# Three first products in quarters, and two more pairs of kept T blocks, in a Strassen-like matmul with leaky ReLU

## The chip, the cores and the metric

One core of one Trainium2 chip runs the whole kernel. The time is device time in microseconds (us) from start to end of one execution; a kernel's time is the median of several executions. One execution is also recorded by the hardware profiler; its span runs from the first to the last instruction.

## The reference

```python
a = randn(4096, 4096) float32;  b = randn(4096, 4096) float32;  alpha = 0.01
x = np.matmul(a, b)
return np.where(x > 0, x, alpha * x)
```

## The kernel before

**Tiling.** Both matrices are cast to 16 bits. `out` is cut into 4 groups of 1024 rows (g) and 4 pairs of 1024 columns (j). A region (g, j) is one 1024x1024 block of `out`, with the inner dimension of 4096 cut in two halves of 2048, each again in two units k = 0, 1 of 1024 (8 chunks of 128 rows). Region (0, 0) is done by plain products. The other 15 run in the order of `regions`: (0, 1), (0, 2), (0, 3), then in each of groups 1 and 2 the pairs 2, 0, 3, 1, and in group 3 the pairs 2, 0, 1, 3. A *turning* region is the last of its group: it also brings in the A blocks of the next one.

**A region** is one step of the Winograd form of Strassen's scheme. A group has the blocks A11, A12, A21, A22 and sums S1 to S4 of them; a pair has B11, B12, B21, B22 and sums T. A block of B is held as two tiles, one for each k, and the name B(half, nt, k) in the code is unit k of it: B11 is (0, 0), B12 (0, 1), B21 (1, 0), B22 (1, 1). The sums T are written over the blocks: T3 = B22 - B12 over B12, T2 = B11 + T3 over B11. `PRODUCTS` (line 667) lists seven products, each 512 rows by 512 columns and 2048 deep:

```python
PRODUCTS = [("a11", 0, 0), ("a12", 1, 0), ("s2", 0, 0), ("s3", 0, 1), ("s1", 0, 0), ("a22", 1, 0), ("s4", 1, 1)]
```

I call them the first to the seventh. A whole product is 64 matmuls with 512 columns (`product`, line 831). The first is written to four banks of the accumulator memory called y, copied by ACT (ScalarE) to four banks z (line 1132), and then the second is added onto z and the third onto y.

**Quarters.** In the regions that are neither the first of a group nor turning, the fifth, fourth, sixth and seventh product (in that order) are split once more by the same scheme: seven `quarter_product` calls (line 770) of 16 matmuls with 256 columns each, 112 in place of 64. Their operands are quarters of the blocks and sums of quarters: on the A side four sums, made once per group by DVE (VectorE) and stored in DRAM (`sums_of_a`, line 719; `kept_q`), and loaded for every region by `load_sums` (line 762), 512 KB each; on the B side sums made by DVE for every region (lines 696 to 706). A sum is held in a tile "q16" of a pool with three buffers or in a quarter of a tile "q", so a load or a DVE sum must wait until the quarter product that read the old content is done.

**The seventh product in quarters** (`seventh_in_quarters`, line 989) issues, in this order, the quarter products of: the block x01, x00, the sum s(4), x11, s(2), s(1), s(3). It reads its accumulators with ACT (lines 999, 1003, 1008) and DVE (lines 1005, 1009, 1011), and `leave` (lines 313, 1076) applies the leaky ReLU on DVE and lets the queue SP (SyncE) store 4 parts of 256 KB.

**Transfers.** B in float32 is fetched and cast by DMAs that POOL (GpSimd) issues (line 547). From the second group on, the blocks with half 1 of pairs 0, 1 and 3 come from DRAM in 16 bits (`kept_half`, line 544, on SP, 1 MB a unit), and all of pair 2 (`kept`, line 542). For pair 2 also T3 and T2 are kept: `move_t` (line 529) stores them in group 1 and loads them in groups 2 and 3, T3 on SP, T2 on ACT's queue after the first product. S2 is kept too and loaded for each region (`load_s2`, line 789). Everything that an engine issues stands in the order of the code; nothing overtakes on a queue. Each DMA of the queues SP and ACT also gets one of eight completion semaphores in turn, and its issue waits until the DMA that had this semaphore before has landed.

At the end of the sixth product's code the next region's B21 is fetched, then stores of the sixth product's result follow, then, after the code of the seventh, B22 of the next region, S2 for k = 1 and the stores of the seventh product's result:

```python
1366            fetch_b(i + 1, [(1, 0)], (1, 0) if in_quarters else ks)     # B21, kept_half, 2 x 1 MB
1367        leave(u2_pairs, 1, 0)                                           # 4 stores on SP
...
1387                kept_c = seventh_in_quarters(*rest)
1388                fetch_b(i + 1, [(1, 1)], (1, 0))                            # B22, kept_half, 2 x 1 MB
1389                new_s(g, "s2")
1390                load_s2(g, 1)
1391                leave(kept_c, 0, 1)
```

**Measures.** Sums of squares of the blocks (`Measure`, lines 231 to 264: four ACT passes and eight steps of DVE) decide at the end whether 16 bits were enough. `EARLY` (line 659) lists which block is measured during the first product of which region.

Of the kernel before, what the change touches and what calls it, by code (L numbers as in the profile page):

```python
# [8 lines left out]
P = 128  # L9
# [28 lines left out]
OTHERS = (0, 3)  # L38

# [9 lines left out]
def kernel(  # L49
# [407 lines left out]
    for i in range(1, len(steps)):  # L457
# [15 lines left out]
        if i == 5:  # L473

            for u, nt in ((u, nt) for u in range(2) for nt in range(2)):
                for c in range(0, KC, 4):
                    load_b(1, u, c, 4, nt)
# [21 lines left out]
        if i == 4:  # L499
            for m in first_columns:  # L500
                m.end()
        if i == 5:
            for mt in range(MT):
                leave_first(h, mt)
        if i == 5:
            first_measure = Measure(0, halves(at[0, 1, 0]) + halves(at[0, 1, 1]), True, room)
            first_measure.begin()
        if i == 6:
            first_measure.end()
# [4 lines left out]
    kept_t = {name: dram_pool.tile([2, P, KC * NT], DT, name=f"kept_{name}") for name in ("t3", "t2")}  # L514
# [12 lines left out]
    def move_t(name, t, k, out, queue=nc.sync):  # L527
        ends = kept_t[name][k], t.rearrange("p c n -> p (c n)")
        queue.dma_start(*(ends if out else ends[::-1]))

    def fetch_unit(i, u, nt, later=False):
# [7 lines left out]
        if g > 1 and j == CACHED and (half, nt) == (0, 1):  # L539
            move_t("t3", t, u, False)  # L540
# [89 lines left out]
    def judge(line):  # L630
# [29 lines left out]
        (1, 3): [B11], (2, 0): [B21], (2, 3): [B21], (2, 1): [B12], (3, 1): [B11, B21],  # L660
# [14 lines left out]
    kept_q = {name: dram_pool.tile([4, P, QUARTER], DT, name=f"kept_q{name}") for name in ("a22", "s4", "s1")}  # L675
    FIFTH = {(1, 0), (1, 3), (2, 0), (2, 3), (3, 0), (3, 1), (3, 3)}
# [123 lines left out]
    in_quarters = False  # L800
    for i, (g, j) in enumerate(regions):
# [6 lines left out]
        ybank = 0 if i % 2 == 0 else 4  # L808
        zbank = 4 - ybank
# [6 lines left out]
        def product(n, banks, first):  # L816
            name, half, nt = PRODUCTS[n]

# [3 lines left out]
            if n == 0 or n == 2 and in_fourth:  # L822
                order[-16:] = [(mt, k, c) for mt in range(MT) for k, c in todo[-4:]]
            elif n == 1 or n == 4 and in_fourth:
                order[:16] = [(mt, k, c) for mt in range(MT) for k, c in todo[:4]]
# [14 lines left out]

        def keep(banks, side):
            pairs, kept = new_c(side)
            for mt in range(MT):
                nc.scalar.copy(kept[mt], banks[mt])  # L844
            return pairs, kept

# [51 lines left out]
        def fifth_in_quarters(y, banks, tq, sx, pairs, between):  # L898
# [6 lines left out]
            onto = lambda r, n: [y[2 * r + m][:, n * HALF:(n + 1) * HALF] for m in range(2)]  # L905
# [6 lines left out]
            def more(r, n, room):  # L912
                for m, to in enumerate(onto(r, n)):
                    nc.vector.tensor_add(to, to, room[:, m])

            quarter_product(x[0, 1], b[1, 0], onto(0, 0))
            quarter_product(x[0, 0], b[0, 0], into(chain), True)
            one = copied(0, 0, chain)
            quarter_product(a_quarter(sx[4]), b[1, 1], onto(0, 1))
# [3 lines left out]
            quarter_product(x[1, 1], t(4), onto(1, 0))  # L923
# [9 lines left out]
            last = copied(1, 1, chain)  # L933
            for m in range(2):
# [3 lines left out]
        def sixth_in_quarters(pairs, banks, v_pairs, v, y, tq, sq):  # L938
# [20 lines left out]
            add(v, y)  # L959
# [28 lines left out]
        def seventh_in_quarters(y, one, other, tq, sq):  # L988
# [7 lines left out]
            onto = lambda r, n: [y[2 * r + m][:, n * HALF:(n + 1) * HALF] for m in range(2)]  # L996
            quarter_product(x[0, 1], b[1, 0], onto(0, 0))
            quarter_product(x[0, 0], b[0, 0], into(one), True)
            nc.scalar.copy(block(0, 0), pair(one))
            quarter_product(sx(4), b[1, 1], onto(0, 1))  # L1000
            quarter_product(x[1, 1], t(4), onto(1, 0))
            quarter_product(sx(2), t(2), into(one))
            nc.scalar.copy(block(0, 1), pair(one))
            quarter_product(sx(1), t(1), into(other), True)
            nc.vector.tensor_add(block(0, 1), pair(other), block(0, 1))
            quarter_product(sx(3), b[0, 1], into(one))
            for n in (1, 0):
                nc.scalar.copy(block(1, n), pair(one))
            nc.vector.tensor_add(block(1, 1), pair(other), block(1, 1))
            for mt in range(MT):  # L1010
                nc.vector.tensor_add(kept[mt], y[mt], kept[mt])
            return pairs

        def seventh_at_the_end(y, one, other, tq, sq, one_more):
# [9 lines left out]
            onto = lambda r, n: [part(y[2 * r + m], n) for m in range(2)]  # L1024
# [8 lines left out]
            for mt in (2, 3):  # L1033
                nc.scalar.copy(part(kept[mt], 1), part(y[mt], 1))
            quarter_product(x[0, 1], b[1, 0], onto(0, 0))
            for mt in range(2):
                more(mt, 0, part(y[mt], 0))
# [7 lines left out]
            quarter_product(sx(4), b[1, 1], onto(0, 1))  # L1045
            for mt in range(2):
                more(mt, 1, part(y[mt], 1))
# [7 lines left out]
            quarter_product(x[1, 1], t(4), onto(1, 0), by_row=True)  # L1055
            for mt in (2, 3):
                more(mt, 0, part(y[mt], 0))
# [53 lines left out]
        y = [new_bank(ybank + mt) for mt in range(MT)]  # L1111
        z = [new_bank(zbank + mt) for mt in range(MT)]
# [6 lines left out]
        in_fifth = (g, j) in FIFTH  # L1119
        second_of_group = in_fourth and regions[i - 2][0] != g  # L1120
        early = [measure(i, *block) for block in EARLY.get((g, j), [])]
        for m in early[:1]:
# [3 lines left out]
        product(0, y, True)  # L1126
        if second_of_group:
            sums_of_s3(g, (2,))
        for m in early[:1]:
            m.end()  # L1130
        for mt in range(MT):
            nc.scalar.copy(z[mt], y[mt])  # L1132
        if second_of_group and g in [of for of, _ in FIFTH]:
            sums_of_a(g, "s1", new_a16)
        for m in early[1:]:
            m.begin()
        have_t2 = g > 1 and j == CACHED
        if have_t2:
            for k in ks:
                t = have_b[i, k, 0] = b_pool.tile([P, KC, NT], DT, name="b", tag="b11")  # L1140
                move_t("t2", t, k, False, nc.scalar)
        if middle:
            middle.begin()
        for k in ks:
            if have_t2:
                break
# [4 lines left out]
            if g == 1 and j == CACHED:  # L1151
                move_t("t3", B(0, 1, k), k, True)
                move_t("t2", B(0, 0, k), k, True)
        if middle:
            middle.end()
        for m in early[1:]:
# [6 lines left out]
        note_rows()  # L1163
        if first_of_group:
            sum_a(g, "s3")
            if g:
                sum_a(g, "s4")
        bring_a(0, 0, range(1 if g else 4))
# [31 lines left out]
        if in_fifth:  # L1200
# [8 lines left out]
        if in_fifth:  # L1209
# [6 lines left out]
        for k in ks:  # L1216
            halves_of = [slice(None)]
            if in_fifth and k == ks[1]:
# [7 lines left out]
            if in_fourth and k == ks[0]:  # L1226
                y7 = quarters_of_b(i, 0, 1)
                t3_of_b(y7)
                if not in_fifth:
                    tq = {n: new_a16() for n in (2, 1)}  # L1230
                    sums_of_b(y7, tq, (2, 1))
# [8 lines left out]
        z = [new_bank(zbank + mt) for mt in range(MT)]  # L1240
# [6 lines left out]
        if in_fourth:  # L1247
            y6 = quarters_of_b(i, 1, 0)
            if in_fifth:
                t5 = {2: t[:, 0], 1: t[:, 1], 4: t[:, 2]}  # L1250
                y5 = quarters_of_b(i, 0, 0)
                t3_of_b(y5)
                sums_of_b(y5, t5)
                tq, sq = {}, {}

                def for_the_fourth():
                    tq[2] = new_a16()
                    sums_of_b(y7, tq, (2,))
                    yield
                    tq[1] = new_a16()  # L1260
                    sums_of_b(y7, tq, (1,))
                    s3_fourth(t[:, 0])
                    yield
                    sq[1] = new_a16()
                    load_sums("a22", sq, (1,))
                    tq[4] = t[:, 2]
                    sums_of_b(y7, tq, (4,))
                    yield

                v_pairs, v = new_c(side)  # L1270
                fifth_in_quarters(y, z, t5, s5, v_pairs, for_the_fourth())
                z = [new_bank(zbank + n) for n in (2, 3, 1, 0)]
                t6 = {2: t[:, 1], 1: t[:, 3], 4: t[:, 2]}
                late = t[:, 0]
            else:
                tq[4], late = t[:, 0], t[:, 3]
# [198 lines left out]
```

## Time and profile before

| | |
|---|---|
| time, median of 3 runs | 1526.23 us (1526.18 to 1531.6) |
| the profiled execution | 1526.13 us |
| its span | 1524.2 us |
| busy: PE (TensorE) | 1512.9 us, 99% |
| busy: DVE | 1166.7 us, 77% |
| busy: ACT | 512.2 us, 34% |
| busy: POOL | 258.3 us, 17% |
| DMA, mean | 244 GB/s |

The busy time of PE is modelled, since matmuls overlap each other; what a matmul costs is read from the distance of starts in a long row of them. Waits of SP are waits of a queue that only issues DMAs.

### The profile page before, as it was taken

To read this page: it belongs to the slowest core of one execution; us is meant where nothing else is said; L and a number is where in the kernel's file an instruction comes from. 1 tells how busy PE (TensorE), PEld (TensorE's weight loads), DVE (VectorE), ACT (ScalarE), POOL (GpSimd) and SP (SyncE) were. 2 spreads that over 40 slices of the span, in tenths; PEclk is the share of its full clock that TensorE was granted. 3 is DMA by queue.
4 is the path that set the end of the run, shared out by engine and by line. 5 is a ranking of instruction groups with operands and counts; after the bars stand their busy time and mean duration, and the time that the engine had idled before them with its cause. 6 is when DMAs were issued, how large, how long until landed. Compare 5 with 4: busy or idle time off the path is not lost.

```text
span 1524.2 us, 22803 instructions
## 1 busy us (share of the span) xinstructions
PE 1512.9 (99%) x9003; PEld 879.2 (58%) x9003; DVE 1166.7 (77%) x1221; ACT 512.2 (34%) x885; POOL 258.3 (17%) x426
## 2 busy tenths in 40 slices
PE   9999999999999999999999999999999999999998
PEld 4444444444446577584544748667554475848667
DVE  4588867666896597777779598777978779888797
ACT  2411535537410123124661132323574113252221
POOL 5641110233202011012320101000331100101000
PEclk9999999999999999999999999999999999999999
DMA  9999995999889999999898968859999894968935
GB/s 247 189 215 206 242 285 164 174 187 193 235 330 247 285 300 288 290 289 271 199 273 317 287 252 187 312 151 330 220 239 313 223 337 148 276 238 205 331 122 172
DMA packets 197767, 372.29 MB, mean 244 GB/s; under 512 B 19345, under 2 KB 132241, under 8 KB 184594
## 3 DMA queue, kind: packets, MB, share of 16 engines
q0 software_dynamic: 119808, 112.22, 46.7%
q1 hardware_dynamic: 71218, 232.95, 41.0%
q10 hardware_dynamic: 6624, 25.56, 4.3%
q8 instruction: 72, 1.18, 0.3%
q14 instruction: 45, 0.37, 0.1%
HBM read 359.66 MB, written 121.11 MB: 315 GB/s over the span
## 4 chain that ended last, share of the span: by engine, by line
PE 58%; DMA 6%; DVE 1%; issue 1%; SPq 0%; POOL 0%; DVEq 0%; POOLq 0%
PE ps L831 34%; PE ps L770 25%; DMA b<-in_b_dram 5%; DMA q<-kept_qs 1%; DVE b L603 0%; DVE c L313 0%; DVE c L1028 0%; POOL b L547 0%; SPq L1076 0%; DVE b L696 0%; DVE b L1225 0%; SPq L762 0%; DVEq L603 0%; DVEq L313 0%; POOLq L547 0%
## 5 line engine op out<-in xcount | busy, mean ns | idle before, releaser
L831 PE MATMUL ps<-b,a 128*128 128x512 f16 x2624 | 570.6, 379 | 0.0
L831 PEld LDWEIGHTS <-a 128*128 128x128 f16 x2624 | 256.7, 98 | 307.8
L831 PE MATMUL ps<-b,s 128*128 128x512 f16 x1792 | 391.3, 379 | 0.0
L831 PEld LDWEIGHTS <-s 128*128 128x128 f16 x1792 | 175.4, 98 | 210.9
L603 DVE TENSOR_TENSOR b<-b 128x4096 f16<-128x4096 f16 x97 | 218.9, 2286 | 51.3 <-DMA b<-in_b_dram 33.1
L547 POOL DMA_DIRECT2D b<-in_b_dram x128 | 94.8, 745 | 870.5 <-PE ps L770 266.1
L770 PEld LDWEIGHTS <-q 128*128 128x128 f16 x1872 | 182.6, 98 | 23.2 <-DMA q<-kept_qs 1.6
L844 ACT COPY c<-ps 128x512 f32<-128x512 f32 x164 | 85.9, 596 | 287.5 <-PE ps L831 277.7
L133 POOL DMA_DIRECT2D a<-in_a_dram x252 | 137.5, 553 | 246.5 <-ACT junk L622 81.3
L142 DVE STREAM_TRANSPOSE a<-a 128x512 uint32<-128x512 uint32 (+2 forms) x120 | 127.0, 1107 | 66.5 <-DMA a<-in_a_dram 66.5
L313 DVE SCALAR_TENSOR_TENSOR c<-c 128x1024 f32<-128x1024 f32 (+2 forms) x123 | 141.9, 1196 | 17.7 <-ACT c L844 17.4
L622 ACT ACTIVATE junk<-a 128x512 bf16<-128x512 f16 x192 | 121.2, 631 | 72.8 <-DMA a<-in_a_dram 67.7
L770 PEld LDWEIGHTS <-a 128*128 128x128 f16 x1200 | 117.4, 98 | 14.7
L231 ACT ACTIVATE sq<-b 128x2048 bf16<-128x2048 f16 x60 | 111.3, 1911 | 43.1 <-DVE sq L240 36.7
L770 PE MATMUL ps<-b,q 128*128 128x256 f16 x1008 | 118.6, 273 | 0.0
L283 PE MATMUL ps<-b,a 128*128 128x512 f16 x512 | 112.2, 379 | 0.5 <-ACT a L380 0.2
L770 PEld LDWEIGHTS <-s 128*128 128x128 f16 x960 | 93.8, 98 | 14.2 <-DVE b L603 1.3
L770 PE MATMUL ps<-q,q 128*128 128x256 f16 x864 | 99.9, 273 | 0.9 <-DMA q<-kept_qs 0.9
L770 PE MATMUL ps<-b,a 128*128 128x256 f16 x752 | 88.3, 273 | 0.0
L283 PEld LDWEIGHTS <-a 128*128 128x128 f16 x512 | 49.7, 98 | 60.8 <-issue 1.4
L1132 ACT COPY ps<-ps 128x512 f32<-128x512 f32 x60 | 32.8, 572 | 147.8 <-PE ps L831 147.8
L1063 DVE TENSOR_TENSOR c<-ps,c 128x512 f32<-128x512 f32 x72 | 44.6, 683 | 47.6 <-PE ps L831 38.0
(125 smaller groups left out, 1053.6 us busy)
## 6 DMA issues: line engine op xcount, KB each, us to landing
b<-in_b_dram POOLq DMA_DIRECT2D x136, 512.0 KB, 12.4
out_dram<-c SPq DMA_DIRECT2D x240, 256.0 KB, 7.8
a<-in_a_dram POOLq DMA_DIRECT2D x244, 128.0 KB, 5.7
b<-kept_half SPq DMA_DIRECT2D x28, 1024.0 KB, 11.8
b<-kept SPq DMA_DIRECT2D x20, 1024.0 KB, 9.2
q<-kept_qs ACTq DMA_DIRECT2D x40, 512.0 KB, 7.2
s<-kept_s SPq DMA_DIRECT2D x18, 1024.0 KB, 9.1
q<-kept_qs SPq DMA_DIRECT2D x28, 512.0 KB, 6.1
```

What stands on the lines that cost most here:

```text
L133: nc.gpsimd.dma_start(a16[32 * q:32 * q + 32], src.rearrange("(g i) w -> i g w", i=32))
L142: nc.vector.transpose(part.rearrange("p c m e -> p c (m e)").bitcast(U32) .rearrange("p c (g i) -> p g c i", i=32), src[:, :, i * n:(i + 1 ...
L231: nc.scalar.activation(to, self.parts[n], SQUARE)
L283: nc.tensor.matmul(ps, a_cols(at[0, h, u], c, mt, (h, u) == (0, 0)), bt[0, u, nt][:, c, :], start=first, stop=last,)
L313: nc.vector.scalar_tensor_tensor(t, t, alpha, t, op0=MULT, op1=MAX if alpha <= 1 else MIN)
L547: nc.gpsimd.dma_start(t[:, c:c + 4, :], b_rows(j, u, c, 4, nt, g > 0))
L603: nc.vector.tensor_tensor(f(to), f(x0), f(x1), op)
L622: nc.scalar.activation(junk, piece[:, q, :], SQUARE, accum_out=to[:, 4 * n + q:4 * n + q + 1])
L770: nc.tensor.matmul(to[m], xq[:, c // 2, rows, c % 2], yq[:, c, :], start=first and c == 0 and m < banks, stop=c == KC - 1, skip_group_chec ...
L831: nc.tensor.matmul(banks[mt], a_cols(t, c, mt, t is first_a), B(half, nt, k)[:, c, :], start=first and (k, c) == todo[0], stop=(k, c) == t ...
L844: nc.scalar.copy(kept[mt], banks[mt])
L1063: nc.vector.tensor_add(to, bank, to)
```

## The change

It has three parts.

1. In the regions (2, 3), (3, 1) and (3, 3) (`FIRST`) the first product, too, is done in quarters, by a new `first_in_quarters`. Its seven quarter products read x00, s(1), s(2), x01, s(3), s(4), x11, with four sums of A11 that `sums_of_a` makes and stores in the first region of groups 2 and 3 (`kept_qa11`). They are loaded, and T3, T2, T1 of quarters of B11 are made, between the quarter products of the seventh product of the region before (`for_the_first`); T4 is made within the first product. In these regions each bank holds one quarter, so the second and third products run as 128 matmuls with 256 columns. S2 for k = 1 is loaded later, after the first product's code. Banks are handed on by lists Y and Z.
2. T3 and T2 of pairs 0 and 3 are kept as well: stored in (2, 0) and (2, 3), loaded in (3, 0) and (3, 3). There the four sums of DVE and the fetch of B12 in float32 fall away.
3. Two measures move: B21 of pair 0 from region (2, 0) to region (0, 0), where the first measure also starts one step earlier, and B11 of pair 1 from (3, 1) to (1, 1).

A list of regions (`FIFTH`) that covered every region with a fourth product in quarters is dropped with the branches it never took.

```diff
+KEPT_T = {CACHED: 1, 0: 2, 3: 2}
...
-        if g > 1 and j == CACHED and (half, nt) == (0, 1):
-            move_t("t3", t, u, False)
+        if g > KEPT_T.get(j, G) and (half, nt) == (0, 1):
+            move_t("t3", j, t, u, False)
...
-        (1, 3): [B11], (2, 0): [B21], (2, 3): [B21], (2, 1): [B12], (3, 1): [B11, B21],
+        (1, 3): [B11], (1, 1): [B11], (2, 3): [B21], (2, 1): [B12], (3, 1): [B21],
...
+    FIRST = {(2, 3), (3, 1), (3, 3)}
...
+        in_first = (g, j) in FIRST
+        if in_first:
+            shared_bank = Z[1]
+            Y, Z = [Z[2], Z[3], Y[0], Z[0]], [Y[1], Y[2], Z[1], Y[3]]
+        else:
+            Y, Z = Z, Y
...
         def product(n, banks, first):
             name, half, nt = PRODUCTS[n]
+            if in_first:
+                for k in ks:
+                    for q in (0, 1, 3, 2):
+                        for c in range(KC):
+                            for m, to in enumerate(into(banks[q])):
+                                nc.tensor.matmul(
+                                    to, a_cols(operand(g, name, k), c, q // 2 * 2 + m),
+                                    B(half, nt, k)[:, c, q % 2 * HALF:(q % 2 + 1) * HALF],
...
+        def for_the_first(tq, sq, first_t, first_s):
+            y1 = quarters_of_b(i + 1, 0, 0)
...
+            first_s[1] = new_a16()
+            load_sums("a11", first_s, (1,))       # after the quarter product of s(4)
+            yield
+            first_s[2] = tq[4]
+            load_sums("a11", first_s, (2,))       # after that of x11
+            yield
+            first_t[3], first_t[2] = new_a16(), tq[2]
+            tt(f(3), y1[1, 1], y1[0, 1], SUB)
+            tt(f(2), f(3), y1[0, 0], ADD)         # after that of s(2)
+            yield
+            first_t[1], first_s[3] = new_a16(), tq[1]
+            tt(f(1), y1[1, 1], f(2), SUB)
+            load_sums("a11", first_s, (3,))       # after that of s(1)
+            yield
+            first_s[4] = sq[3]
+            load_sums("a11", first_s, (4,))       # after that of s(3)
+            yield
+
+        def first_in_quarters(y, shared, z, tq, sq):
+            room = new_c(side)[0][1][:, :, :HALF]
+            b = quarters_of_b(i, 0, 0)
+            x = quarters_of_a(g, "a11")
+            one, other, third, chain = y
...
+            quarter_product(x[0, 0], b[0, 0], into(chain), True)
+            nc.scalar.copy(one, chain)
+            quarter_product(sx(1), t(1), into(shared), True)
+            nc.scalar.copy(room, pair(shared))
+            tq[4] = new_a16()
+            nc.vector.tensor_tensor(t(4), b[1, 0], t(2), SUB)
+            quarter_product(sx(2), t(2), into(chain))
+            nc.scalar.copy(other, chain)
+            quarter_product(x[0, 1], b[1, 0], into(one))
+            nc.scalar.copy(z[0], one)
+            quarter_product(sx(3), t(3), into(chain))
+            nc.scalar.copy(third, chain)
+            nc.vector.tensor_add(pair(chain), pair(chain), room)
+            quarter_product(sx(4), b[1, 1], into(other))
+            nc.vector.tensor_add(pair(other), pair(other), room)
+            quarter_product(x[1, 1], t(4), into(third))
+            z[2] = new_bank(Z[2])
+            for to, bank in ((3, chain), (1, other), (2, third)):
+                nc.scalar.copy(z[to], bank)
...
-                kept_c = seventh_in_quarters(*rest)
+                first_t, first_s = {}, {}
+                between = for_the_first(tq, sq, first_t, first_s) if next_first else nothing()
+                kept_c = seventh_in_quarters(*rest, between)
                 fetch_b(i + 1, [(1, 1)], (1, 0))
-                new_s(g, "s2")
-                load_s2(g, 1)
+                if not next_first:
+                    new_s(g, "s2")
+                    load_s2(g, 1)
                 leave(kept_c, 0, 1)
```

The remarks behind `load_sums` and `tt` are not in the code.

226 lines of the change are left out of this document (131 added, 95 removed).

## The prediction, on record before the run

> **What bounds the kernel now.** I read the page first, then the chain of waits, then PE's and SP's waits, then the timeline of one place. PE is the bound: it has work in every slice, and the chain's second half is nothing else.
>
> ```profile
> PE 1512.9 (99%) x9003; PEld 879.2 (58%) x9003; DVE 1166.7 (77%) x1221; ACT 512.2 (34%) x885; POOL 258.3 (17%) x426
> ```
>
> In the chain (start, length, what) one region, here (2, 3), is two rows: the first three products, 192 matmuls with 512 columns, then four products in quarters, 448 with 256.
>
> ```profile
> 967.10 41.44 PE ps L831 x192
> 1008.54 48.91 PE ps L770 x448
> ```
>
> A matmul takes 41.44 / 192 = 0.2158 us with 512 columns and 48.91 / 448 = 0.1092 us with 256, 1.2% more than half. So a product costs 13.81 us whole, 112 x 0.1092 = 12.23 us in seven quarters, and one quarter product 1.75 us. Nearly nothing of PE's time is waiting: its longest wait for a transfer is 0.9 us.
>
> ```profile
> PE ps L770 <- DMA q<-kept_qs: 0.9, 1, 0.9
> ```
>
> Only what shortens PE's work or makes PE wait can move the time. What DVE, ACT and POOL save is worth nothing.
>
> **What PE saves.** In three regions the first product falls from 64 to 112 half-size matmuls, and the second and third go from 64 to 128 each: 112 + 128 + 128 = 368, x 0.1092 = 40.17 us, against 41.44. That is 1.27 us a region, **3.8 us** in all. More cannot come from it.
>
> **What PE must now wait for.** The new first product needs sums of A11 from DRAM, s(1) for its second quarter product, 1.75 us after it starts, s(2), s(3), s(4) at the third, fifth and sixth. Their loads stand on SP behind the fetch of B21 and four stores, and they take their turn in the eight semaphores. Here is that queue of before in the last products of (2, 0) and of (3, 0), from B21's fetch (L544 x2) over the stores (L1076) to B22's (L544 again), which stands where s(1) will stand.
>
> ```profile
> 951.41 4.12 SPq L544 DMA_DIRECT2D b<-kept_half  x2
> 958.59 5.12 SPq L1076 DMA_DIRECT2D out_dram<-c  x4
> 966.64 0.81 SPq L544 DMA_DIRECT2D b<-kept_half  x2
> ...
> 1320.73 3.88 SPq L544 DMA_DIRECT2D b<-kept_half  x2
> 1336.07 0.87 SPq L544 DMA_DIRECT2D b<-kept_half  x2
> ```
>
> B22 is issued at 966.64 though the buffers' last reader may end later; what released it is B21's first half, eight DMAs earlier on the same semaphore, as the tile b's answers for single issues show (time of issue, then issue to landing): 951.4 + 15.2 = 966.6.
>
> ```profile
> L544 SPq DMA_DIRECT2D b<-kept_half x1: 412/412/412, 951.4 to 951.4; - x1
> DMA to landing us min/median/max: 15.2/15.2/15.2
> ...
> L544 SPq DMA_DIRECT2D b<-kept_half x1: 326/326/326, 966.6 to 966.6; - x1
> DMA to landing us min/median/max: 9.3/9.3/9.3
> ...
> L544 SPq DMA_DIRECT2D b<-kept_half x1: 327/327/327, 967.1 to 967.1; - x1
> DMA to landing us min/median/max: 11.2/11.2/11.2
> ...
> L544 SPq DMA_DIRECT2D b<-kept_half x1: 411/411/411, 1320.7 to 1320.7; - x1
> DMA to landing us min/median/max: 15.3/15.3/15.3
> ...
> L544 SPq DMA_DIRECT2D b<-kept_half x1: 327/327/327, 1336.1 to 1336.1; - x1
> DMA to landing us min/median/max: 9.6/9.6/9.6
> ```
>
> SP's waits name this releaser seven times, up to 3.9 us.
>
> ```profile
> SPq L544 <- DMA b<-kept_half: 20.5, 7, 3.9
> ```
>
> In the changed program the load of s(1) is the eighth after B21's first half, on the same semaphore. Its buffer is free early, at the end of the quarter product of s(4) (959.95 below), so the semaphore decides: issue at 966.64. The landing lies between 6.1 us, the quickest row of such a load on SP, and the 9.3 us of the whole megabyte issued then.
>
> ```profile
> L762 SPq DMA_DIRECT2D q<-kept_qa x1: 319/319/319, 940.9 to 940.9; - x1
> DMA to landing us min/median/max: 6.1/6.1/6.1
> ```
>
> The first megabyte landed at 975.9, the second at 967.1 + 11.2 = 978.3: 2.4 us each once the stores ahead are out. Half a megabyte lands 1.2 us before the first, at 974.7. PE asks for it at:
>
> ```profile
> 958.20 1.91 PE L770 MATMUL ps<-b,q 128*128 128x256 f16 x16
> 959.95 1.91 PE L770 MATMUL ps<-q,s 128*128 128x256 f16 x16
> 965.19 1.91 PE L770 MATMUL ps<-b,q 128*128 128x256 f16 x16
> 966.93 3.40 PE L831 MATMUL ps<-b,a 128*128 128x512 f16 x15
> ...
> 1336.25 4.05 PE L831 MATMUL ps<-b,a 128*128 128x512 f16 x18
> ```
>
> The first product begins at 966.93, its second quarter product 1.75 later, at 968.7. PE waits 974.7 - 968.7 = **6.0 us** (4.0 to 7.2). In (3, 1) it is 1336.1 + 9.6 - 1.2 = 1344.5 against 1338.0: **6.5 us** (4.2 to 7.7). s(2) and s(3) follow 1.2 us apart, s(4) when B21's second half has landed; after such a wait all come before PE does.
>
> The third place, before (3, 3), differs. B12 of that region comes as T3, 2 MB on SP in place of POOL's fetch in float32, whose last pieces take up to 30.9 us and so are in flight until B21 has landed.
>
> ```profile
> L547 POOL DMA_DIRECT2D b<-in_b_dram x2: 742/746/750, 941.2 to 941.9; - x2
> DMA to landing us min/median/max: 24.9/27.9/30.9
> ```
>
> Without them I let B21's first half land in 9.3 us instead of 15.2, s(1) be issued 9.3 after it, at 960.7 on the clock of (2, 0), and land 6.1 to 8.2 us later, at 966.8 to 968.9 against 968.7: **0**, and up to 6 if the fetch isn't what slows B21.
>
> The Trainium skill (DMA: Bandwidth & Descriptors, "Queues, rings and completion order") says that each engine takes descriptors of one ring in order, which agrees with B22's landing behind the stores; by it half a megabyte behind them cannot come at 6.1.
>
> **The clock after the wait.** PE starts the kernel with 11 matmuls of 512 columns in 4.75 us, 0.43 each, half speed; after that waits of up to 0.9 us cost no clock, by the page's row of the granted clock (9 is 90% or more).
>
> ```profile
> PEclk9999999999999999999999999999999999999999
> ...
> 1.19 4.75 PE L106 MATMUL wp<-w 128*128 128x512 f16 x11 [1.19 <-DVE x L92]
> ```
>
> No row shows a wait of 6 us. Between nothing and a cold start like this one, which loses 4.75 / 2 = 2.4 us, I take the middle, 1.2 us a wait, **2.4 us** for two. The Trainium skill (TensorE: Matmul & The Clock Gate, "Part 1: The HAM clock gate") has PE fall to half its clock after an idle window of some 3.4 us and need as long a busy one to rise: by that rule every such wait costs clock, some 1.7 us as an estimate from its figure.
>
> **What I cost at nothing.** DVE gains T3, T2, T1, T4, 1.22 us each (row below), and two adds in each of the three regions. T3 and T2 fit into its 5.74 us of idling before L1005; T1 waits for the quarter product of s(1), done at 965.2, and is ready 2 us later, against 968.7. Were that cover gone, each T would add 1.2 us.
>
> ```profile
> L702 DVE TENSOR_TENSOR q<-b 128x2048 f16<-128x2048 f16 x36 | 44.0, 1224 | 5.8 <-PE ps L831 4.8
> 965.44 0.69 DVE L1005 TENSOR_TENSOR c<-ps,c 128x512 f32<-128x512 f32 x1 [5.74 <-issue]
> 851.69 2.48 DVE L1063 TENSOR_TENSOR c<-ps,c 128x512 f32<-128x512 f32 x4 [10.35 <-PE ps L831]
> ```
>
> The sums of A11 in (2, 2) and (3, 2) are four more such steps, 4.9 us, ahead of idling of 10.35 us; their stores join SP's queue there, in front of stores only. The stores of T3 and T2 in (2, 0) and (2, 3), 1 MB each, stand ahead of the loads of S1's sums and use their semaphores, but land within about 12 us, before the fifth product asks, two products after they start. The loads in (3, 0) and (3, 3) take 5.8 to 12.3 us by the kept T rows of pair 2 and T2 has the second product, 13.8 us; if it came late the price is 1 to 3 us a place.
>
> ```profile
> DMA to landing us min/median/max: 5.8/10.0/12.3
> ```
>
> S2 for k = 1 now leaves some 11 us later; its product starts 26 us after the first. The measures keep their number: in (1, 1) DVE idles 5.72 us waiting for B22 where the added one comes, and in region (0, 0) it idles 5.29 us before the transposes.
>
> ```profile
> 699.85 2.29 DVE L603 TENSOR_TENSOR b<-b 128x4096 f16<-128x4096 f16 x1 [5.72 <-DMA b<-kept_half]
> 86.92 2.09 DVE L142 STREAM_TRANSPOSE a<-a 128x512 uint32<-128x512 uint32 x2 [5.29 <-DMA a<-in_a_dram]
> ```
>
> A measure needs some 6.5 us of DVE, so each of these two shifts work by about 1 us, and PE waits for neither.
>
> **The sum.** The profiled execution took 1526.13 us, the median of the runs is 1526.23, so it stands for them. 1526.13 - 3.8 + 6.0 + 6.5 + 0 + 2.4 = **1537.2 us**, and with waits of 5 to 7 us each and 0.6 to 2.4 us of clock for each, 1533.5 to 1541.1. What a measurement of this kernel can tell from no change is about 0.5%, 7.6 us: below 1518.6 is faster, above 1533.8 slower.
>
> **The rivals.** *No wait* (chance 0.15): the loads come in time everywhere, because B21 lands sooner or another DMA's semaphore is the one that counts. Then 1526.1 - 3.8 = 1522.3, not slower. Against it: to be in time s(1) must be issued by 968.7 - 6.1 = 962.6, that is B21's first half must land in 11.2 us, not 15.2; from that point this rival decides. *Short waits* (0.17): s(1) lands in its quickest 6.1 us, the clock holds, 4.0 + 4.2: 1530.5. *Full cold starts* (0.10): each wait costs clock like the kernel's own start, 2.4 instead of 1.2: 1539.6. It is what the rule of the clock gate named above would do. *All three wait* (0.13): (3, 3) waits like (3, 1), 6 + 1.2 more: 1544.4. *The saving isn't there, or something costed at nothing shows* (0.05): quarters that load every weight twice run slower, or T2 comes late; the 448 matmuls of the chain row speak against the first. 1526.1 + 12.5 + 2.4 = 1541. The forecast keeps 0.40.
>
> **How the numbers follow.** Slower: forecast 0.39, cold starts, three waits and the last rival 0.28, together 0.67. Within 0.5%: no wait, short waits and the forecast's edge, 0.32. Faster by over 0.5% would need 7.6 us where PE's work shrinks by 3.8: 0.01. The range must hold 8 in 10, and leaving out the case of no wait with the upper tail would leave out more, so it reaches from 1522 to 1545; the likeliest case's own is 1533 to 1541.
>
> **What would show it.** PE's waits: a new row "PE ps <- DMA q<-kept_qa", two waits of about 6 us, at the second quarter product of the first product of (2, 3) and (3, 1), none or a small one in (3, 3). SP: the load of s(1) issued as B21's first half lands. The chain: 112 matmuls in 12.2 us plus the wait, and the granted clock dipping behind it. If PE's waits stay under 1 us, I am wrong at the semaphores; if the waits are there but sit at s(3) or s(4), at which load is late.

## The result, and the profile after

The changed kernel took 1540.61 us (median of 4 runs, 1537.5 to 1541.11) against 1526.31 for the kernel before on the same chip: ratio 1.0085, 95% interval 1.0071 to 1.0099, so slower by 14.3 us (the interval is 10.8 to 15.1) where the sum of the prediction's terms gave 11.1. The profiled execution took 1540.35 us, its span is 1538.5.

The page's busy times of the changed kernel: PE's sum has grown by 2.0 us only, so most of the time went into waits.

```profile
PE 1514.9 (98%) x9531; PEld 933.1 (61%) x9531; DVE 1175.2 (76%) x1227; ACT 518.1 (34%) x897; POOL 252.2 (16%) x418
```

PE's waits in the changed kernel (us in total, times, longest). The first row is new; it was named in the prediction. The ACT row is new too, and was not.

```profile
PE ps L775 <- DMA q<-kept_qa: 11.1, 2, 5.7
PE ps L775 <- DVE b L608: 1.8, 1, 1.8
...
PE ps L775 <- ACT c L875: 0.6, 3, 0.2
PE ps L775 <- DMA q<-kept_qs: 0.5, 1, 0.5
```

PE's timeline of the changed kernel at the first products of (2, 3) and (3, 1). The first row of each place is the quarter product of x00, the next that of s(1), then s(2); the bracket is the idle time ahead and what ended it.

```profile
968.22 1.91 PE L775 MATMUL ps<-b,a 128*128 128x256 f16 x16
975.83 3.59 PE L775 MATMUL ps<-q,q 128*128 128x256 f16 x16 [5.70 <-DMA q<-kept_qa]
979.22 2.89 PE L775 MATMUL ps<-q 128*128 128x256 f16 x16
981.94 1.91 PE L775 MATMUL ps<-b,a 128*128 128x256 f16 x16
...
1345.32 1.91 PE L775 MATMUL ps<-b,a 128*128 128x256 f16 x16
1352.62 3.59 PE L775 MATMUL ps<-q,q 128*128 128x256 f16 x16 [5.39 <-DMA q<-kept_qa]
1356.01 2.25 PE L775 MATMUL ps<-q 128*128 128x256 f16 x16
1358.09 1.91 PE L775 MATMUL ps<-b,a 128*128 128x256 f16 x16
```

By the distance of starts the waits are 975.83 - 968.22 - 1.75 = 5.86 us and 1352.62 - 1345.32 - 1.75 = 5.55. Behind them two quarter products take 6.11 us and 5.47 where 3.50 is the full speed: 2.61 and 1.97 us of clock. The windows of the trace say it outright; the first column in brackets counts PE's matmuls, and the column behind POOL's busy time is the granted clock:

```profile
973.00:974.30 1.30, 0.00 (x0) 0.00 (x0) 1.30 (x2) 0.00 (x0) 0.00 (x0) 1.00 1.07 418
974.40:981.20 6.80, 5.37 (x26) 3.82 (x27) 1.42 (x2) 0.58 (x1) 0.00 (x0) 0.50 1.03 425
981.30:985.00 3.70, 3.70 (x36) 3.31 (x34) 0.00 (x0) 1.14 (x2) 0.00 (x0) 1.00 0.95 370
```

The clock is halved for some 6.8 us, from inside the wait on. PE works in 5.37 us of them, and half of that, 2.7 us, is about the loss. In (3, 1) the clock is halved from 1349.9 to 1356.6, and PE works in 3.98 us of it.

SP's queue in the changed kernel (start, time over which the group was issued), ahead of (2, 3) and then of (3, 3):

```profile
952.72 3.80 SPq L549 DMA_DIRECT2D b<-kept_half  x2
959.88 5.10 SPq L1178 DMA_DIRECT2D out_dram<-c  x4
967.95 3.56 SPq L767 DMA_DIRECT2D q<-kept_qa  x4
...
1426.63 4.88 SPq L549 DMA_DIRECT2D b<-kept_half  x2
1433.59 2.02 SPq L1178 DMA_DIRECT2D out_dram<-c  x4
1436.66 6.43 SPq L767 DMA_DIRECT2D q<-kept_qa  x4
```

And the landing of B21's first half there, from the groups of its line in two windows of the same kernel, (2, 3) and (3, 3):

```profile
DMA to landing us min/median/max: 15.2/15.2/15.2
...
DMA to landing us min/median/max: 10.0/10.0/10.0
```

952.72 + 15.2 = 967.9 and 1426.63 + 10.0 = 1436.6: at both places s(1) is issued when B21's first half lands, as the semaphores' turn would have it. In (3, 3) that is early enough; the first product there begins at 1442.58, and no wait for q<-kept_qa follows. It is early enough by very little: the load took 7.7 us to land, to 1444.4, and the quarter product of s(1) starts at 1444.45, 0.12 us later than at full rate.

PE's timeline of the changed kernel once more: where the fifth products of (2, 3), (3, 1) and (3, 3) start, which is the end of the first three products, and the start of the first product of (3, 3).

```profile
1016.88 3.66 PE L775 MATMUL ps<-b,s 128*128 128x256 f16 x32
...
1393.02 3.66 PE L775 MATMUL ps<-b,s 128*128 128x256 f16 x32
...
1442.58 1.91 PE L775 MATMUL ps<-b,a 128*128 128x256 f16 x16
1444.45 1.92 PE L775 MATMUL ps<-q,q 128*128 128x256 f16 x16
...
1482.89 3.66 PE L775 MATMUL ps<-b,s 128*128 128x256 f16 x32
```

### The profile page after: what moved, and what is told of

The parts are those of the page before. It is cut to its first block, busy times and chain, and to the rows that moved or that the text cites. A ratio compares the mean times of both kernels' runs of the same rounds, so it can differ in the third digit from the quotient of the medians.

```text
span 1538.5 us, 23936 instructions
## 1 busy us (share of the span) xinstructions
PE 1514.9 (98%) x9531; PEld 933.1 (61%) x9531; DVE 1175.2 (76%) x1227; ACT 518.1 (34%) x897; POOL 252.2 (16%) x418
## 4 chain that ended last, share of the span: by engine, by line
PE 54%; DMA 9%; DVE 1%; issue 1%; SPq 0%; ACT 0%; POOL 0%; DVEq 0%; POOLq 0%; ACTq 0%
PE ps L775 24%; PE ps L852 24%; PE ps L833 5%; DMA b<-in_b_dram 3%; DMA b<-kept_half 2%; DMA q<-kept_qs 1%; DMA q<-kept_qa 1%; DMA kept_half<-b 1%; DVE c L314 0%; DMA out_dram<-c 0%; DVE b L608 0%; ACT c L875 0%; SPq L1178 0%; DVE c L880 0%; DVE c L1170 0%
## 5 line engine op out<-in xcount | busy, mean ns | idle before, releaser
L852 PE MATMUL ps<-b,a 128*128 128x512 f16 x2240 | 487.2, 379 | 0.0
L852 PEld LDWEIGHTS <-a 128*128 128x128 f16 x2240 | 219.1, 98 | 263.1
L852 PE MATMUL ps<-b,s 128*128 128x512 f16 x1600 | 349.6, 379 | 0.0
L852 PEld LDWEIGHTS <-s 128*128 128x128 f16 x1600 | 156.6, 98 | 188.5 <-issue 0.3
L608 DVE TENSOR_TENSOR b<-b 128x4096 f16<-128x4096 f16 x89 | 200.7, 2285 | 42.9 <-DMA b<-in_b_dram 37.2
L775 PEld LDWEIGHTS <-q 128*128 128x128 f16 x2064 | 203.7, 99 | 38.9 <-DMA q<-kept_qa 11.9
L875 ACT COPY c<-ps 128x512 f32<-128x512 f32 x164 | 84.9, 596 | 283.1 <-PE ps L852 203.6
L775 PEld LDWEIGHTS <-a 128*128 128x128 f16 x1344 | 131.5, 98 | 16.3
L775 PE MATMUL ps<-q,q 128*128 128x256 f16 x960 | 114.7, 277 | 11.3 <-DMA q<-kept_qa 11.1
L284 PE MATMUL ps<-b,a 128*128 128x512 f16 x512 | 112.2, 379 | 0.5 <-ACT a L381 0.2
L775 PEld LDWEIGHTS <-s 128*128 128x128 f16 x960 | 93.8, 98 | 16.4 <-DVE b L608 2.8
L775 PE MATMUL ps<-b,a 128*128 128x256 f16 x848 | 99.8, 273 | 0.0
L284 PEld LDWEIGHTS <-a 128*128 128x128 f16 x512 | 49.7, 98 | 60.8 <-issue 1.4
L1242 ACT COPY ps<-ps 128x512 f32<-128x512 f32 x48 | 26.4, 572 | 121.6 <-PE ps L852 121.5
L775 PE MATMUL ps<-b,s 128*128 128x256 f16 x544 | 63.0, 273 | 2.9 <-DVE b L608 1.8
```

What stands on the lines that cost most here:

```text
L284: nc.tensor.matmul(ps, a_cols(at[0, h, u], c, mt, (h, u) == (0, 0)), bt[0, u, nt][:, c, :], start=first, stop=last,)
L608: nc.vector.tensor_tensor(f(to), f(x0), f(x1), op)
L775: nc.tensor.matmul(to[m], xq[:, c // 2, rows, c % 2], yq[:, c, :], start=first and c == 0 and m < banks, stop=c == KC - 1, skip_group_chec ...
L852: nc.tensor.matmul(banks[mt], a_cols(t, c, mt, t is first_a), B(half, nt, k)[:, c, :], start=first and (k, c) == todo[0], stop=(k, c) == t ...
L875: nc.scalar.copy(to, bank)
```

## The experiments

Each time stands with its ratio to the kernel before, measured beside it on the same chip. Remarks behind # in the cuts are not in the code.

**Another queue.** Is it SP's order or the shared semaphore? The four loads of A11's sums go to ACT's queue; the place of s(1) in the semaphores' turn is the same.

```diff
-            load_sums("a11", first_s, (1,))
+            load_sums("a11", first_s, (1,), nc.scalar)      # and so for (2,), (3,), (4,)
```

> The four loads of A11's sums are issued by ACT's queue instead of SP's; bytes, place in the order of the eight semaphores and everything else stay, so the load of s(1) still takes its turn behind the first half of B21, but no longer stands behind the four stores on SP. Theory (the semaphore holds it): still issued when B21's first half lands, some 15 us after that one's issue, PE still waits 4 to 6 us in (2, 3) and in (3, 1) and loses clock behind it, 1536 to 1542 us. Rival (its place on SP behind the stores holds it): issued when its buffer is free, some 7 us sooner, PE waits under 1 us, 1523 to 1527 us.

It took 1542.92 us (1.0124, 1.0107 to 1.0140), slower than the changed kernel and just above the expected range. ACT's timeline of this kernel, ahead of (2, 3):

```profile
969.56 0.83 ACTq L767 DMA_DIRECT2D q<-kept_qa  x2
970.44 0.59 ACT L1046 COPY c<-ps 128x512 f32<-128x512 f32 x1 [8.49 <-DVE q L1080]
```

PE's timeline of the same stretch:

```profile
971.08 1.91 PE L775 MATMUL ps<-b,q 128*128 128x256 f16 x16 [2.77 <-ACT c L1046]
...
979.36 1.92 PE L775 MATMUL ps<-q 128*128 128x256 f16 x16 [0.98 <-DMA q<-kept_qa]
```

The load is issued no earlier, at 969.56, which is again 15.2 us after B21's first half (954.38 in this kernel), though nothing but ACT's own work is ahead of it now. Its issue holds ACT, so ACT's copy of the accumulator comes at 970.44, right behind the two issues, after 8.49 us of idling in place of 4.66 in the changed kernel; PE waits for that copy inside the seventh product, and then for the load as well. The bracket names a step of DVE that ended at the same moment. In (3, 1) that step ended at 1346.83, and the copy came at 1347.70, again right behind the issues (DVE's row, then ACT's):

```profile
1345.60 1.23 DVE L1080 TENSOR_TENSOR q<-b,q 128x2048 f16<-128x2048 f16 x1
...
1346.02 1.64 ACTq L767 DMA_DIRECT2D q<-kept_qa  x2
1347.70 0.59 ACT L1046 COPY c<-ps 128x512 f32<-128x512 f32 x1 [8.90 <-DVE q L1080]
```

SP's order alone is refuted as the cause.

**B21 out of the turn.** The fetch of B21 goes behind the seventh product's code for the three regions, so that it is no longer eight DMAs ahead of s(1).

```diff
-            fetch_b(i + 1, [(1, 0)], (1, 0) if in_quarters else ks)
+            if not next_first:
+                fetch_b(i + 1, [(1, 0)], (1, 0) if in_quarters else ks)
...
                 kept_c = seventh_in_quarters(*rest, between)
+                if next_first:
+                    fetch_b(i + 1, [(1, 0)], (1, 0))
```

> Same queue and same bytes as the changed kernel, but ahead of the three regions B21's fetch (2 MB) stands behind the loads of A11's sums instead of in front of the stores, so s(1) takes a semaphore that was free long before. Theory (the semaphore holds it): s(1) issued at about the end of the quarter product of s(4), 6 to 7 us sooner, PE waits 0 to 1 us at it, no clock lost: 1540.6 - 11.4 (two waits) - 4.6 (slow matmuls behind them) = 1524.6, 1523 to 1528 us, faster than before by up to 3 us. Rival (the transfers are simply too many at that place, bandwidth): waits stay near 6 us, 1536 to 1541 us. Rival (the wait moves to B21, now fetched late, at the second product): 1527 to 1533 us with a wait of PE on kept_half.

1527.0 us (1.0006, 0.9997 to 1.0014), 1.3 above before in place of 14.3, by moving one fetch; the interval does not tell it from before. SP's issue of the loads ahead of (2, 3) in this kernel; then, on PE's timeline, the same place as above and, in (3, 3), the third product:

```profile
963.25 6.76 SPq L767 DMA_DIRECT2D q<-kept_qa  x4
...
972.41 1.92 PE L775 MATMUL ps<-q,q 128*128 128x256 f16 x16 [1.01 <-DVE c L880]
...
1456.68 14.15 PE L833 MATMUL ps<-b,s 128*128 128x256 f16 x128 [1.28 <-DMA s<-kept_s]
```

The load of s(1) is issued at 963.25 in place of 967.95. It then takes 9.1 us to land, more than the 7.8 in the changed kernel, so it is the earlier issue that helps and not a lighter load on the DMA engines. It lands at 972.4, which is what PE's wait of 1.01 us ends on, though the bracket names DVE: PE's weight load waited 1.3 us for it.

A new wait has come in (3, 3): S2's issue on SP waited 7.0 us for a half of B's landing (the row of SP's waits: SPq L794 <- DMA b<-kept_half, 7.0). It is the same turn, with another load in the eighth place. The result is 2.4 us above what was expected; the waits left at the three places, 1.01, 0.49 in (3, 1) and 1.28 us, come to 2.8.

**The change without the first products.** `FIRST` is empty; the kept T blocks and the moved measures stay.

```diff
-    FIRST = {(2, 3), (3, 1), (3, 3)}
+    FIRST = set()
```

> The second and third part of the change alone: T3 and T2 of pairs 0 and 3 kept, two measures moved, all first products whole. Theory: off PE's path, 1526.3 with 1.5 either way, PE waits as before. Rival (their transfers or the measures are part of the 14 us): 1529 us or more, with a wait of PE at (1, 0), (2, 0), (3, 0) or (3, 3).

1529.35 us (1.0027, 1.0017 to 1.0037), 3 us more than expected of what I had costed at nothing. PE's timeline has a gap of 0.22 us behind ACT's copies (L875) at the start of five fifth products, none of which is in the trace of before. One line of the diff, which neither I nor the section on the change above had named, makes them. The kernel before issued the last 16 matmuls of the third product bank by bank, so that ACT could copy the first banks while PE filled the last; the change drops that:

```diff
-            if n == 0 or n == 2 and in_fourth:
+            if n == 0:
                 order[-16:] = [(mt, k, c) for mt in range(MT) for k, c in todo[-4:]]
```

**The dropped order, taken back and taken alone.** The kernel of the last run with the left line of this diff again; and the kernel before with only this diff. (In the first of the two the same condition also got into `fetch_a`, which runs only in turning regions, where it is never true.)

> No first product in quarters; T3 and T2 of pairs 0 and 3 kept and the measures moved, as in the changed kernel; but the last 16 matmuls of the third product are issued bank by bank again. The kernel without this line took 1529.35 us against 1525.68 for before, and its fifth products began with gaps of 0.22 us behind ACT's copies of the third product's banks. Theory: the dropped order is what costs, since all four banks end with the product's last matmuls and ACT copies the first of them 2.4 us later than before: about 1526.0 us (1525.0 to 1527.5), gaps of 0.22 gone. Rival: the kept T blocks or the moved measures cost: 1529 (1528 to 1530.5).

> The kernel before with one edit: the last 16 matmuls of the third product are no longer issued bank by bank. Theory (the dropped order is what costs): slower than before by 2.5 to 3.7 us, about 1528.8 us, with gaps of 0.2 to 0.4 us at the start of the fifth products. Rival (kept T blocks or measures): as before, 1525.7 us, within 0.7 us.

1526.43 us (1.0008, 0.9999 to 1.0017) and 1528.82 us (1.0018, 1.0009 to 1.0027). So it is the order, and the kept T blocks and the moved measures cost nothing that can be seen. Here is the chain of the second kernel, around (2, 3):

```profile
919.40 48.96 PE ps L770 x447
...
1010.32 48.96 PE ps L770 x447
```

From one fifth product to the next are 1010.32 - 919.40 = 90.92 us; before (in the prediction's rows) it is 41.44 + 48.91 = 90.35. That is 0.57 us a region. The line bears on seven regions when `FIRST` is empty, but only the five from (2, 0) on show the loss, 2.8 us together, against the 2.7 between the medians of the second kernel and before; in (1, 0) and (1, 3) PE waits for other things at that place as well, in one kernel or the other. Of the five, the changed kernel has two left, (2, 0) and (3, 0).

**Is it the wait that costs the clock?** 24 matmuls of 512 columns, whose result nothing uses, fill the time between the first and the second quarter product.

```diff
             nc.scalar.copy(one, chain)
+            for n in range(24):
+                nc.tensor.matmul(shared, a_cols(operand(g, "a11", n % 2), n % KC, n % MT), B(0, 0, n % 2)[:, n % KC, :],
+                                 start=True, stop=True, skip_group_check=True)
             quarter_product(sx(1), t(1), into(shared), True)
```

> The changed kernel with 24 matmuls of 512 columns that go to a bank that is cleared afterwards, between the first and the second quarter product of the three new first products: 24 x 0.216 = 5.2 us of work in which PE would wait in two of them, and 5.2 us more work in (3, 3). Theory (the clock falls in the wait): in (2, 3) and (3, 1) the quarter products behind run at 1.75 us instead of 3.4 and 2.1 to 2.7, 4.6 us less, and (3, 3) costs 5.2 more: about 1541.2 us; the place to look is the length of the second quarter product. Rival (these two are slow because their operands land late): they stay at 3.4 and 2.1 to 2.7, about 1545.8 us.

1542.58 us (1.0117, 1.0103 to 1.0132). PE's timeline of this kernel in (2, 3):

```profile
971.39 5.34 PE L1099 MATMUL ps<-b,a 128*128 128x512 f16 x24
976.91 1.92 PE L775 MATMUL ps<-q,q 128*128 128x256 f16 x16 [0.18 <-DMA q<-kept_qa]
978.67 1.91 PE L775 MATMUL ps<-q 128*128 128x256 f16 x16
```

The load still decides the start, 976.91, but the quarter products run at once at 1.75 us from start to start. The longer quarter products of the changed kernel were the price of the idle time, not of the loads going on beside them; the granted clock of the window 971:983 is 1.00. The total isn't lower because (3, 3), which doesn't wait, pays for the 24 matmuls too.

**The third place.** T3 and T2 are kept for pair 2 only, so POOL fetches B12 of (3, 3) in float32 again.

```diff
-KEPT_T = {CACHED: 1, 0: 2, 3: 2}
+KEPT_T = {CACHED: 1}
```

> The changed kernel with T3 and T2 kept for pair 2 alone, as before: B12 of (3, 3) is fetched in float32 by POOL again. Theory (the third place was free because the float32 fetch was gone, so that the first half of B21 landed early): a wait of about 5.5 us for q<-kept_qa at the second quarter product of (3, 3), 2.0 to 2.6 us of clock behind it, together some 8 us more than the changed kernel: 1548 us (1545 to 1550). Rival (the third place is free for another reason): no such wait, 1540.6 us (1539 to 1542).

1548.09 us (1.0148, 1.0132 to 1.0163), as expected. SP's queue in this kernel at (3, 3):

```profile
1425.67 3.88 SPq L549 DMA_DIRECT2D b<-kept_half  x2
...
1441.02 3.40 SPq L767 DMA_DIRECT2D q<-kept_qa  x4
```

And PE's timeline:

```profile
1448.06 3.50 PE L775 MATMUL ps<-q,q 128*128 128x256 f16 x16 [4.76 <-DMA q<-kept_qa]
```

With the float32 fetch s(1) is issued 15.35 us after B21's first half (1441.02 - 1425.67) in place of 10.0, and (3, 3) waits like the others. The second part of the change is what spared the third place.

**The order back in the changed kernel.** The changed kernel with one line turned back.

```diff
-            if n == 0:
+            if n == 0 or n == 2 and in_fourth:
```

> The changed kernel with one edit: the last 16 matmuls of the third product are issued bank by bank again where the products are whole, which is (1, 0), (1, 3), (2, 0) and (3, 0). Theory: 0.57 us a region (the distance of starts of two such regions was 90.92 us without this order and 90.35 with it), 4 regions, 2.3 us less than the changed kernel: 1538.3 us (1537 to 1539.5), the waits for q<-kept_qa unchanged. Rival (the waits absorb it, since the loads' times are set by their queue and not by PE): 1540.6 us.

1540.04 us (1.0088, 1.0074 to 1.0102): between the two expectations, and nearer to the rival's. The two waits grew, to 6.27 and 6.01 us in place of 5.70 and 5.39, by as much as the order gains in (2, 0) and (3, 0): the loads landed by their queue's time, as the rival had it. The intervals of the two kernels overlap, and I take no more from it.

**Versions that should beat both.** First B21 behind everywhere, the order back, and S2's load between B21 and B22, where its turn is harmless, in place of behind the first product.

```diff
                 if next_first:
                     fetch_b(i + 1, [(1, 0)], (1, 0))
+                    new_s(g, "s2")
+                    load_s2(g, 1)
                 fetch_b(i + 1, [(1, 1)], (1, 0))
```

> The kernel with B21's fetch behind the seventh product's sums (1527.0 us), with two more edits: S2 for k = 1 is fetched between B21 and B22 in place of behind the first product, so that its issue no longer has B21's first half on its semaphore (it made the third product of (3, 3) wait 1.28 us); and the last 16 matmuls of the third product are issued bank by bank again. Theory: 1527.0 - 1.3 - 1.7 (the dropped order's 3 us in seven regions, four of which are left here) = 1524.0 us (1523 to 1525.5), faster than before by some 1.7 us. Rival (what is left goes to new waits of DVE and B22): 1526.5 us or more.

1542.77 us (1.0114, 1.0099 to 1.0130), a plain miss. The name in the expectation was a mistake as well: in the run with B21 out of the turn, S2's issue had waited for B22's first half, not B21's. SP's queue in this kernel ahead of (2, 3):

```profile
968.23 0.90 SPq L549 DMA_DIRECT2D b<-kept_half  x2
979.66 0.32 SPq L794 DMA_DIRECT2D s<-kept_s  x1
980.03 0.90 SPq L549 DMA_DIRECT2D b<-kept_half  x2
```

DVE's timeline, at the first step of T3:

```profile
987.03 2.29 DVE L608 TENSOR_TENSOR b<-b 128x4096 f16<-128x4096 f16 x1 [6.66 <-DMA b<-kept_half]
```

And PE's, at the start of the fifth product:

```profile
1012.27 1.92 PE L775 MATMUL ps<-b,s 128*128 128x256 f16 x16 [2.95 <-DVE b L608]
```

S2's buffer still holds operands of the first product's quarters. Its issue waits 10.5 us for the quarter products that read them, and B22, behind it on SP, waits with it. DVE makes T3 late, all its later work is late, and PE pays 25 us further on, at the fifth product. What is behind a waiting issue had to be asked here too, and I had not asked it.

Next, the order still back, S2 again behind the first product, and B21 behind for (2, 3) and (3, 1) only.

```diff
+        behind = next_first and regions[i + 1] != (3, 3)       # takes the place of next_first at B21's fetch
```

> The changed kernel with two edits: B21's fetch stands behind the loads of A11's sums for (2, 3) and (3, 1) only, and stays where it was for (3, 3), where no wait was seen and where S2's load then has B21's first half no longer eight ahead of it; and the last 16 matmuls of the third product are issued bank by bank again. S2's load stays behind the first product. Theory: 1526.1 - 3.8 (the quarters' saving) + 1.0 + 0.5 (the small waits that were left at (2, 3) and (3, 1) with B21 behind) + 0.3 for (3, 3) = 1524.1 us (1523.0 to 1525.3), below before by some 2 us. Rival (the quarters save less than the matmul rate says, or waits of that size come elsewhere): 1526 us or more.

1527.26 us (1.0008, 0.9998 to 1.0017), on the rival's side. PE's timeline of this kernel in (2, 3), at the quarter product of s(1):

```profile
971.78 1.92 PE L775 MATMUL ps<-q,q 128*128 128x256 f16 x16 [1.59 <-DMA q<-kept_qa]
```

Waits of 1.59 us here, 1.16 for s(1) in (3, 1), and 0.84 for S4's sums in the seventh product of (3, 1) are left, 3.6 in all, and they eat what the quarters save. s(1) is now issued at 962.04, when the stores ahead and the quarter product of s(4), the last reader of its buffer, are done, and then it needs 9.7 us to land. So, last, that quarter product one place earlier, and the sixth product's four stores behind the load of s(1):

```diff
+            if behind:
+                quarter_product(sx(4), b[1, 1], onto(y, 0, 1))      # ahead of x00 in place of behind it
+                next(between)
             quarter_product(x[0, 0], b[0, 0], into(one), True)
```

> The kernel of the run before last (B21 behind for (2, 3) and (3, 1), the order of the third product back) with two more edits for these two places: in the seventh product before, the quarter product of s(4) goes ahead of that of x00, so that the buffer for s(1) is free 1.75 us sooner, and the four stores of the sixth product's result stand behind the load of s(1) in place of ahead of it. Theory (with the turn out of the way, the buffer and these stores set when s(1) is issued, at 962.0 in (2, 3); a load then lands 6.3 to 9.7 us later, and PE asks 8.2 us after the issue): issued some 1.7 us sooner, the waits of 1.59 and 1.16 us fall below 0.4 each, 2.0 to 2.5 us less: 1.5 to 2.5 us below before, ratio 0.9985. Rival (the later s(2) and s(3) or the delayed stores then hold PE): no gain, ratio 1.0000 to 1.0010.

1525.04 us (0.9995, 0.9986 to 1.0004). SP's queue ahead of (2, 3):

```profile
958.23 0.33 SPq L767 DMA_DIRECT2D q<-kept_qa  x1
...
963.32 3.97 SPq L767 DMA_DIRECT2D q<-kept_qa  x3
```

And PE's timeline, now at the quarter product of s(2):

```profile
971.49 1.92 PE L775 MATMUL ps<-q 128*128 128x256 f16 x16 [1.06 <-DMA q<-kept_qa]
```

s(1) is in time. The wait has moved to s(2) (1.06 and, in (3, 1), 0.68 us), which is issued at 963.32 and lands 8.1 us later (7.8 in (3, 1)). The median is 1.4 us below before, which the interval does not tell from no change.

## Why the prediction was right, and where its sizes were off

**The mechanism** is shown: the load of s(1) is issued when B21's first half lands, on whichever of the two queues it stands, and taking B21 out of the turn takes the waits away. The two waits came where they were expected, 5.86 and 5.55 us for 6.0 and 6.5; in (3, 1) the load landed 7.5 us after its issue, where I had 8.4.

**The third place** was right too, and for the reason given: 10.0 us of landing for 9.3, the issue at 1436.66, no wait; with the float32 fetch back it waits. But s(1) landed there without a margin; that the wait was 0.12 us and not 1 is luck.

**The saving** was right. From first to fifth product, the first three products of (2, 3) take 1016.88 - 968.22 = 48.66 us; less 5.86 and 2.61 that is 40.19, where the prediction has 40.17 and before 41.44. (3, 1) gives 40.18, and (3, 3) 1482.89 - 1442.58 = 40.31 with the 0.12 us at s(1). That is 3.64 us saved in place of 3.8.

**The clock** was undersized: 2.61 and 1.97 us, 4.6 together, where I took 2.4. The middle between nothing and a cold start was the wrong choice; the row of the cold start (2.4) was the nearer one, and the rival with full cold starts, to which I gave 0.10, has the sum nearest to the result, 1539.6. That it comes so near is in part luck, since the waits' 1.1 us less and the 1.2 us of the dropped order cancel.

**What was costed at nothing.** T's stores and loads, the measures and the sums of A11 did cost nothing visible. The sums were not tested alone; the 736 matmuls of (2, 2) and around it, beside which the first of them are made, take as long as before (110.51 and 24.45 us in both chains). The line I had not seen in the diff cost 0.57 us a region, and the load of S4's sums in (3, 1)'s seventh product came late for PE, by 0.47 us in its row and 0.65 by the distance of starts.

The terms against before are, then: waits 11.4, clock 4.6, dropped order in (2, 0) and (3, 0) 1.2, S4's sums 0.65, saving -3.64: 14.2. Up to the start of (2, 0) the changed kernel was 0.67 us behind. On the way there it waits 1.81 us for DVE b L608 at the fifth product of (1, 0), and before 0.56. The kernel with `FIRST` empty, which has the same code up to there, waits 0.70, so that is what two executions differ by, and I don't put it on the change. Behind the last of the new first products the changed kernel gains 0.55 us, whose cause stays open. The spans differ by 14.3.

So of the 3.2 us between the forecast's 11.1 and these 14.3, clock and dropped order are 3.4; the waits' 1.1 less and S4's 0.65 and the saving's 0.16 more nearly cancel.

## What to carry to other kernels

When loads share completion semaphores in turn, look for the DMA that stands eight places ahead of an urgent load: if that is a large one, the small one starts only when it has landed, and moving the large one behind was worth 13 us here. When the load is moved instead, ask for the queue it goes to what stands behind it while it waits, for its buffer or its semaphore: ACT's copies in one run here, B22 in another. And read every line of a diff that touches an issue order, even one in the middle of a clean-up: one condition dropped was worth 0.57 us a region on an engine that is 99% busy.

## What the runs showed of the hardware

Whether the clock fell depended on the length of the idle time, and it turned between two neighbouring lengths. In the runs above, PE's idle gaps of 2.77 us (loads on ACT's queue) and 2.95 us (S2 between B21 and B22) were followed by a quarter product of 1.91 and 1.92 us by its row, as everywhere. Behind gaps of 3.46 and 3.60 us they took longer. PE's timeline of the kernel with S2 between B21 and B22, in (3, 1):

```profile
1386.18 5.21 PE L775 MATMUL ps<-b,s 128*128 128x256 f16 x32 [3.46 <-DVE b L608]
1391.22 1.91 PE L775 MATMUL ps<-b,q 128*128 128x256 f16 x16
```

And that of the kernel with the loads on ACT's queue:

```profile
1348.33 2.83 PE L775 MATMUL ps<-b,q 128*128 128x256 f16 x16 [3.60 <-ACT c L1046]
...
1353.49 1.91 PE L775 MATMUL ps<-q,q 128*128 128x256 f16 x16
```

Two quarter products took 5.04 and 5.16 us in place of 3.50, a loss of 1.5 and 1.7 us, against 2.0 and 2.6 behind the gaps of 5.4 and 5.7 us. The Trainium skill (TensorE: Matmul & The Clock Gate, "Part 1: The HAM clock gate") has the clock halve after an idle window of about 3.4 us, and full speed back after a busy one; these four gaps agree with the first, and the granted clock of 0.50 behind the longest wait with the half.

How much a wait loses is set by the part of the halved stretch in which PE works, more than by the wait's own length. Behind the gap of 3.46 us the granted clock is 0.50 for 3.4 us (1386.0 to 1389.4), of which PE works 3.18; behind those of 5.70 and 5.39 us it is 0.50 for some 6.8 us, beginning about 4.3 and 2.6 us after PE has run dry, so once sooner than 3.4. In (3, 3) of the kernel with S2 between B21 and B22, a gap of 5.28 us lost only 1.3 us, since the stretch was again 3.4 us long and began before PE's work. Over all runs here, the waits of 3.46 us and more cost 1.3 to 2.9 us of matmul time on top of themselves.
